# Borders and landing place of the last pieces of a streaming load, moved to multiples of 512 bytes

## The chip, the cores and the metric

One core of one Trainium2 chip. The time is the device time of one execution in microseconds (us). Differences here are far below 2%, so besides times I read landing events (when a transfer's semaphore is full) and packet records (bytes, start and duration of each DMA packet) of the traces, and compare two profiles of one kernel first.

## The reference

```python
x = np.random.randn(32, 512, 1024).astype(np.float32)      # 64 MB
out = np.sum(np.maximum(x, 0), axis=-1)                     # 32 x 512 sums
```

## The kernel before

The 16384 rows of 1024 numbers are spread over 128 partitions, 128 rows each. Loads stream into a buffer of three places of 16 rows; ScalarE applies the maximum, VectorE sums, and for the last rows both do maximum and sum in one instruction per row. What matters here is the end: rows come in transfers of 8, 4 and 2, and the last two rows are cut into four pieces.

```python
buf = nc.alloc_sbuf_tensor("buf", [P, NB, BIG, D], fp32)      # starts at byte 16512 of a partition
w = D - CUT                                                    # CUT = 912, HEAD = 256
seam = nc.alloc_sbuf_tensor("seam", [P, 2 + w + HEAD + 2], fp32)
...
first, second, third = [(0, CUT), (D + D // 2, 2 * D), (D + HEAD, D + D // 2)]
for k, (lo, hi) in enumerate((first, second, third)):
    sp.dma_start(out=flat[:, lo:hi], in_=rows[:, lo:hi]).then_inc(...)
sp.dma_start(out=seam[:, 2 : 2 + w + HEAD], in_=rows[:, CUT : D + HEAD]).then_inc(s_seam, 16)
...
on_act(flat[:, lo : CUT // 2], seam[:, 0:1]).then_inc(s_half, 1)      # halves of the first piece
on_dve(flat[:, CUT // 2 : hi], seam[:, 1:2]).then_inc(s_half, 1)
...                                                                    # second: ScalarE; third: VectorE
act.wait_ge(s_seam, 16 + 2)                                            # seam landed, both others summed
act.wait_ge(s_half, 2)
on_act(seam[:, 0:k], res[:, J - 2 : J - 1]).then_inc(s_last, 1)        # k = 2 + w
dve.wait_ge(s_seam, 16 + 2)
on_dve(seam[:, k : k + HEAD + 2], res[:, J - 1 : J]).then_inc(s_last, 1)
```

The seam holds the end of the last row but one and the start of the last row, with the partial sums of the other pieces in the columns beside them, so that one instruction for each row closes its sum. Then the last store goes out. In the build the big buffer starts 128 bytes past a multiple of 512 (16512 = 32 x 512 + 128), and so does the seam tensor (213120); the seam's data starts two columns later, at byte 136 of a block.

Of the kernel before, what the change touches and what calls it, by code (L numbers as in the profile page):

```python
# [3 lines left out]
P = 128  # L4
D = 1024
# [4 lines left out]
ACT_STEPS = [[16], [7, 9], [7, 9], [7, 9], [4, 5, 7], [3, 4, 5]]  # L10
DVE_STEPS = [[4, 5, 7], [7, 4, 5], [7, 4, 5], [7, 4, 5], [4, 5, 7], [3, 4, 5]]
TAIL = [8, 4, 2]
CUT = 912
HEAD = 256


def bass_relu_sum_kernel(
# [14 lines left out]
    fp32 = mybir.dt.float32  # L32
# [5 lines left out]
    J = B * S // P  # L38
# [11 lines left out]

    buf = nc.alloc_sbuf_tensor("buf", [P, NB, BIG, D], fp32)
    w = D - CUT
    seam = nc.alloc_sbuf_tensor("seam", [P, 2 + w + HEAD + 2], fp32)
    res = nc.alloc_sbuf_tensor("res", [P, J], fp32)
    turned = nc.alloc_sbuf_tensor("turned", [P, 32], fp32)

# [6 lines left out]
    s_half = nc.alloc_semaphore("s_half")  # L63
    s_seam = nc.alloc_semaphore("s_seam")
    s_last = nc.alloc_semaphore("s_last")
# [4 lines left out]
    sp, act, dve = nc.sync, nc.scalar, nc.vector  # L70
# [14 lines left out]
    for c in range(NBIG + 1):  # L85
        if c >= NB:
            sp.wait_ge(s_dve, done[c - NB])
        if c < NBIG:
            i = 0
            for g, j, n in CHUNKS[c]:  # L90
                sp.dma_start(  # L91
                    out=buf[:, c % NB, i : i + n, :], in_=xv[g][:, j : j + n, :]
# [14 lines left out]

    rows = xv[-1].rearrange("p j d -> p (j d)")[:, r * D : (r + 2) * D]
    flat = buf[:, tb, r : r + 2, :].rearrange("p j d -> p (j d)")
    first, second, third = [(0, CUT), (D + D // 2, 2 * D), (D + HEAD, D + D // 2)]  # L110
    for k, (lo, hi) in enumerate((first, second, third)):
        sp.dma_start(out=flat[:, lo:hi], in_=rows[:, lo:hi]).then_inc(  # L112
            s_in[NBIG + len(TAIL) + k], 16
        )
    sp.dma_start(out=seam[:, 2 : 2 + w + HEAD], in_=rows[:, CUT : D + HEAD]).then_inc(s_seam, 16)
    sp.wait_ge(s_turn, 1)
    sp.dma_start(
        out=of[0:P].rearrange("(k q) -> k q", q=32), in_=turned[0:P:32, 0:32]
# [7 lines left out]
    def on_act(t, acc):  # L126
        return act.activation(t, t, AF.Relu, accum_out=acc)  # L127

    def on_dve(t, acc):
        return dve.tensor_scalar(  # L130
            out=t, in0=t, scalar1=0.0, scalar2=None, op0=ALU.max, op1=ALU.add, accum_out=acc
        )
# [4 lines left out]
    k = 0  # L137
    for c in range(NTWO):
# [17 lines left out]
        for n in DVE_STEPS[c]:  # L156
            if ready[r + n - 1] > seen:
# [3 lines left out]
                out=res[:, c * BIG + r : c * BIG + r + n],  # L161
                in_=buf[:, c % NB, r : r + n, :],
# [24 lines left out]
    lo, hi = first  # L187
    act.wait_ge(s_in[-3], 16)
    dve.wait_ge(s_in[-3], 16)
    on_act(flat[:, lo : CUT // 2], seam[:, 0:1]).then_inc(s_half, 1)  # L190
    on_dve(flat[:, CUT // 2 : hi], seam[:, 1:2]).then_inc(s_half, 1)
    k = 2 + w
    lo, hi = second
    act.wait_ge(s_in[-2], 16)
    on_act(flat[:, lo:hi], seam[:, k + HEAD : k + HEAD + 1]).then_inc(s_seam, 1)
    lo, hi = third
    dve.wait_ge(s_in[-1], 16)
    on_dve(flat[:, lo:hi], seam[:, k + HEAD + 1 : k + HEAD + 2]).then_inc(s_seam, 1)
    act.wait_ge(s_seam, 16 + 2)
    act.wait_ge(s_half, 2)  # L200
    on_act(seam[:, 0:k], res[:, J - 2 : J - 1]).then_inc(s_last, 1)
    dve.wait_ge(s_seam, 16 + 2)
    on_dve(seam[:, k : k + HEAD + 2], res[:, J - 1 : J]).then_inc(s_last, 1)

# [33 lines left out]
```

## Time and profile before

The median is 160.83 us. In the trace:

| transfer (issue order) | bytes per partition | landed at, us | from the last packet's end to the landing, us |
|---|---|---|---|
| 4 rows | 16384 | 152.301 | 0.42 |
| 2 rows | 8192 | 154.814 | 0.48 |
| first piece | 3648 | 155.934 | 0.48 |
| second piece | 2048 | 156.626 | 0.53 |
| third piece | 1024 | 156.988 | 0.55 |
| seam | 1472 | 157.438 | 0.47 |
| last store | 64 | 159.349 | 0.38 |

A packet record ends when the engine has done with the packet; the landing is what the program waits for. The distance between the two is 0.42 to 0.55 us for the first five loads and 0.47 us for the seam. The chain of waits and the last instructions are shown in the prediction.

### The profile page before, as it was taken

What the parts mean: (1) busy time and instruction counts of PE and PEld (TensorE: products, weight loads), DVE (VectorE), ACT (ScalarE), POOL (GpSimd) and SP (SyncE); (2) the same over time, 40 slices, a digit from 0 to 9 for tenths busy, and PEclk for the clock granted to TensorE, in tenths of its full rate; (3) what the DMA queues carried; (4) which work ended last, traced back from release to release, by engine and by line L of the source; (5) the groups of instructions that cost most, each with busy time, mean ns of one, the idle gap of its engine ahead of it and who ended that gap; (6) DMA issues with size and microseconds to landing.
All of it is one profiled execution on the core that took longest, in us unless ns stands there. A gap on an engine that the chain in (4) does not pass through costs nothing.

```text
span 159.4 us, 150 instructions
## 1 busy us (share of the span) xinstructions
DVE 120.6 (76%) x59; ACT 101.5 (64%) x54; POOL 0.2 (0%) x4
## 2 busy tenths in 40 slices
DVE  0000000009999999999999999999999999898995
ACT  3000059980799708996099941999329980496975
POOL 0000000000000000000000000000000000000000
DMA  9997996996996997989979969969969979798994
GB/s 378 493 401 339 493 526 263 526 526 263 526 493 296 526 444 345 526 378 411 526 312 477 526 263 526 526 263 526 526 263 526 444 345 526 321 469 374 417 400 142
DMA packets 2457, 67.18 MB, mean 421 GB/s; under 512 B 536, under 2 KB 792, under 8 KB 1176
## 3 DMA queue, kind: packets, MB, share of 16 engines
q1 hardware_dynamic: 2456, 67.18, 98.1%
q14 instruction: 1, 0.01, 0.0%
HBM read 67.11 MB, written 0.07 MB: 421 GB/s over the span
## 4 chain that ended last, share of the span: by engine, by line
DVE 55%; DMA 34%; ACT 9%; SPq 2%; issue 0%
DVE res L160 54%; DMA buf<-in_x_dram 34%; ACT buf L145 9%; SPq L101 1%; SPq L112 1%; DVE buf L130 0%; DVE seam L130 0%; SPq L91 0%; DVE turned L169 0%
## 5 line engine op out<-in xcount | busy, mean ns | idle before, releaser
L160 DVE TENSOR_REDUCE res<-buf 128x4 f32<-128x4096 f32 (+3 forms) x18 | 99.4, 5596 | 35.5 <-ACT buf L145 35.5
L145 ACT ACTIVATE buf<-buf 128x7168 f32<-128x7168 f32 (+5 forms) x13 | 80.4, 6233 | 46.1 <-DMA buf<-in_x_dram 46.1
L127 ACT ACTIVATE buf<-buf 128x1024 f32<-128x1024 f32 (+2 forms) x19 | 19.0, 999 | 8.9 <-DMA buf<-in_x_dram 8.9
L130 DVE TENSOR_SCALAR_CACHE_REDUCE buf<-buf 128x1024 f32<-128x1024 f32 (+2 forms) x19 | 20.7, 1143 | 1.7 <-DMA buf<-in_x_dram 1.6
L127 ACT ACTIVATION_READ_ACCUMULATOR buf<-buf 128x1 f32 x19 | 3.6, 188 | 0.0
L145 ACT ACT_TABLE_LOAD x1 | 1.3, 1283 | 1.3 <-PEq L223 1.3
L130 DVE DVE_READ_ACCUMULATOR buf<-buf 128x1 f32 x19 | 1.6, 84 | 0.0
L130 DVE TENSOR_SCALAR_CACHE_REDUCE seam<-seam 128x258 f32<-128x258 f32 x1 | 0.4, 421 | 0.0
L127 ACT ACTIVATE seam<-seam 128x114 f32<-128x114 f32 x1 | 0.3, 300 | 0.1
L169 DVE STREAM_TRANSPOSE turned<-res 128x32 f32<-128x32 f32 x1 | 0.2, 211 | 0.0
L127 ACT ACTIVATION_READ_ACCUMULATOR seam<-seam 128x1 f32 x1 | 0.2, 186 | 0.0
L223 POOL MEMSET const-bfloat16-1.0<- 128x1 bf16 x1 | 0.1, 101 | 0.0
L223 POOL MEMSET const-uint8-127<- 128x1 uint8 x1 | 0.1, 101 | 0.0
L223 POOL MEMSET const-float32-0.0<- 128x1 f32 x1 | 0.1, 98 | 0.2 <-issue 0.2
L223 POOL MEMSET const-float32-1.0<- 128x1 f32 x1 | 0.1, 98 | 0.0
L130 DVE DVE_READ_ACCUMULATOR seam<-seam 128x1 f32 x1 | 0.1, 82 | 0.0
## 6 DMA issues: line engine op xcount, KB each, us to landing
buf<-in_x_dram SPq DMA_DIRECT2D x1, 7680.0 KB, 21.1
buf<-in_x_dram SPq DMA_DIRECT2D x1, 4096.0 KB, 25.3
buf<-in_x_dram SPq DMA_DIRECT2D x1, 2048.0 KB, 29.9
buf<-in_x_dram SPq DMA_DIRECT2D x1, 1024.0 KB, 31.9
buf<-in_x_dram SPq DMA_DIRECT2D x1, 512.0 KB, 3.3
buf<-in_x_dram SPq DMA_DIRECT2D x1, 456.0 KB, 32.5
buf<-in_x_dram SPq DMA_DIRECT2D x1, 256.0 KB, 32.7
seam<-in_x_dram SPq DMA_DIRECT2D x1, 184.0 KB, 32.6
```

The costliest lines, as they stand in the source:

```text
L101: sp.dma_start(out=buf[:, tb, r : r + n, :], in_=xv[-1][:, r : r + n, :]).then_inc(s_in[NBIG + i], 16)
L112: sp.dma_start(out=flat[:, lo:hi], in_=rows[:, lo:hi]).then_inc(s_in[NBIG + len(TAIL) + k], 16)
L127: return act.activation(t, t, AF.Relu, accum_out=acc)
L130: return dve.tensor_scalar(out=t, in0=t, scalar1=0.0, scalar2=None, op0=ALU.max, op1=ALU.add, accum_out=acc)
L145: act.activation(t, t, AF.Relu).then_inc(s_act, 1)
L160: dve.tensor_reduce(out=res[:, c * BIG + r : c * BIG + r + n], in_=buf[:, c % NB, r : r + n, :], axis=X, op=ALU.add,).then_inc(s_dve, 1)
L169: dve.transpose(out=turned[:, :], in_=res[:, 0:32]).then_inc(s_turn, 1)
L223: nc = _bacc.Bacc("TRN2", target_bir_lowering=False, num_devices=1)
```

## The change

The intent: let every piece of the last two rows begin and end at a multiple of 512 bytes in memory, and let the seam land on one, its partial sums just in front of it (96 columns are 384 bytes, and 128 + 384 = 512).

```diff
-CUT = 912
+CUT = 896
 HEAD = 256
+MID = 512
...
-    seam = nc.alloc_sbuf_tensor("seam", [P, 2 + w + HEAD + 2], fp32)
+    z = 96
+    seam = nc.alloc_sbuf_tensor("seam", [P, z + w + HEAD + 2], fp32)
...
-    first, second, third = [(0, CUT), (D + D // 2, 2 * D), (D + HEAD, D + D // 2)]
+    first, second, third = [(0, CUT), (D + MID, 2 * D), (D + HEAD, D + MID)]
...
-    sp.dma_start(out=seam[:, 2 : 2 + w + HEAD], in_=rows[:, CUT : D + HEAD]).then_inc(s_seam, 16)
+    sp.dma_start(out=seam[:, z : z + w + HEAD], in_=rows[:, CUT : D + HEAD]).then_inc(s_seam, 16)
...
-    on_act(flat[:, lo : CUT // 2], seam[:, 0:1]).then_inc(s_half, 1)
-    on_dve(flat[:, CUT // 2 : hi], seam[:, 1:2]).then_inc(s_half, 1)
-    k = 2 + w
+    on_act(flat[:, lo : CUT // 2], seam[:, z - 2 : z - 1]).then_inc(s_half, 1)
+    on_dve(flat[:, CUT // 2 : hi], seam[:, z - 1 : z]).then_inc(s_half, 1)
+    k = z + w
...
-    on_act(seam[:, 0:k], res[:, J - 2 : J - 1]).then_inc(s_last, 1)
+    on_act(seam[:, z - 2 : k], res[:, J - 2 : J - 1]).then_inc(s_last, 1)
```

## The prediction

> **What bounds the kernel now.** I read the page first (parts 1, 2 and 3), then the chain of waits, then the DMA issues, then the instructions of the last microseconds in order of time, and at last the trace's packet records, landing by landing.
>
> ```profile
> span 159.4 us, 150 instructions
> DVE 120.6 (76%) x59; ACT 101.5 (64%) x54; POOL 0.2 (0%) x4
> DMA packets 2457, 67.18 MB, mean 421 GB/s; under 512 B 536, under 2 KB 792, under 8 KB 1176
> q1 hardware_dynamic: 2456, 67.18, 98.1%
> ```
>
> The reader is to see that the 16 DMA engines are busy for 98.1% of the span and neither compute engine for more than 76%. The kernel is one long load. Only the end, after the last bytes have come, can be shortened by arranging things, and the end is all that the change touches. The packet counts say more than they seem to: 536 packets under 512 B are 276 four-byte semaphore writes, 128 of 64 B and 128 of 444 B (stores) and 4 of 128 B; adding 128 of 1024 B and 128 of 1472 B gives 792; adding 128 each of 2048, 3648 and 4096 B gives 1176. So the 3648-byte piece and the 1472-byte piece each go as one packet per partition. They aren't cut at 512-byte borders, and there is no short remainder packet for the change to remove.
>
> The chain of waits, cut to the last stretch:
>
> ```profile
> 5 pieces in order of time: start us, us, what
> 124.39 32.60 DMA buf<-in_x_dram
> 156.99 0.02 issue
> 157.01 0.44 DVE buf L130 x2
> 157.45 0.02 issue
> 157.47 0.43 DVE seam L130 x2
> ```
>
> It names the 256-column piece (the one of 1024 B per partition, third of four): it lands at 156.99, VectorE reduces it until 157.44, then the last two reductions start. The chain hides a near tie. In the landing events of the trace the 1472-byte "seam" piece, issued last, lands at 157.438 us, and VectorE's third piece ends at 157.442. The final reductions wait for both. Whoever speeds up one alone gains 4 ns and no more.
>
> The last instructions in order of time:
>
> ```profile
> 157.01 0.42 DVE L130 TENSOR_SCALAR_CACHE_REDUCE buf<-buf 128x256 f32<-128x256 f32 x1 [0.40 <-DMA buf<-in_x_dram]
> 157.08 0.34 SPq L123 DMA_DIRECT2D out_dram<-res  x1
> 157.19 0.19 ACT L127 ACTIVATION_READ_ACCUMULATOR buf<-buf 128x1 f32 x1
> 157.36 0.08 DVE L130 DVE_READ_ACCUMULATOR buf<-buf 128x1 f32 x1
> 157.47 0.30 ACT L127 ACTIVATE seam<-seam 128x114 f32<-128x114 f32 x1
> 157.47 0.42 DVE L130 TENSOR_SCALAR_CACHE_REDUCE seam<-seam 128x258 f32<-128x258 f32 x1
> 157.68 0.19 ACT L127 ACTIVATION_READ_ACCUMULATOR seam<-seam 128x1 f32 x1
> 157.82 0.08 DVE L130 DVE_READ_ACCUMULATOR seam<-seam 128x1 f32 x1
> 157.93 0.34 SPq L207 DMA_DIRECT2D out_dram<-res  x1
> ```
>
> ScalarE's final sum ends at 157.87, VectorE's at 157.90; the store is issued at 157.93 and lands at 159.35, 1.42 us later. After that nothing is left.
>
> **What the Trainium skill says, and whether the trace agrees.** "DMA: Bandwidth & Descriptors", section "Specifications", gives 512 B as the smallest transfer at line rate, with read-modify-write below it. That is a size, and all four pieces are above it before and after; only the stores (64 B and 444 B per partition) are below. Section "How a descriptor splits into AXI transactions" of the same page says that a descriptor is cut at 256-byte borders, that a beat is 32 B, and that one which starts off such a border also fetches the bytes back to it. This is the only stated mechanism by which the change can help. The packet records let it be tested below. Section "Anatomy of one DMA — SWDGE (gpsimd) path" puts most of a fixed 2 us into the receipt of the last write. Here the queue is another one, and from the last data packet's end to the last semaphore increment I find 0.42 us (packets of 16384 B), 0.48 (3648 B), 0.53 (2048 B), 0.55 (1024 B) and 0.47 (1472 B): the misaligned piece pays no longer receipt than its neighbours. "SBUF — State Buffer", section "Operand start alignment", says of odd start addresses only that they are legal, and that nothing was timed.
>
> **The change, part by part.** No instruction, wait or transfer is added or removed on any engine; the comparison of instruction orders shows the same 23, 18 and 13 rows on VectorE, ScalarE and the queue, with only sizes changed (456 to 448 twice, 114 to 130, 912 to 896, 368 to 384).
>
> 1. The first piece goes from 3648 to 3584 B per partition, the seam from 1472 to 1536: the same bytes in all. A long packet costs per byte (2418 - 309 ns) / (65536 - 8192 B) = 0.0368 ns on its engine. I divide the time between the ends of successive pieces by the 8 packets that each engine moves of each: 1.116 us / 8 = 139.5 ns for 3648 B, 0.647 / 8 = 80.9 for 2048, 0.344 / 8 = 43.0 for 1024, 0.526 / 8 = 65.8 for 1472. Taking off the bytes (134.2, 75.3, 37.7, 54.1) leaves 5.3, 5.6, 5.3 and 11.7 ns. So three pieces have a fixed part of 5.4 ns, the 3648-byte one among them, although its end is off any 512-byte border; only the seam pays more, about 6.3 ns a packet. The skill's beats agree with that size: the seam is written from byte 136 of a 512-byte block (the tensor starts at 128 of one in the build, and two columns are kept free), which taken from the border below makes 51 beats instead of 46, and 5 beats of 32 B at 0.0368 ns/B are 5.9 ns. They don't explain all: the pieces in the big buffer also land at byte 128 of a block, and pay nothing that can be told from their fixed part.
>
> 2. So the first piece ends 8 x 64 B x 0.0368 = 19 ns sooner, and the second and third with it: the third lands at 156.97. The seam itself has 19 ns more bytes and 8 x 6.3 = 50 ns less of excess: it lands at 157.438 - 0.050 = 157.39.
>
> 3. VectorE's third piece starts 19 ns earlier and, with 0.44 us as before, ends at 157.42. The seam is now 30 ns ahead of it, so the gain on the path is VectorE's 19 ns, not the 50 of the transfer. The last reductions start at 157.45.
>
> 4. VectorE's half of the first piece loses 8 columns and ScalarE's too, some 7 ns each; both had ended well before the third piece landed (156.6). Nothing on the path.
>
> 5. The final sums: VectorE keeps 258 columns (0.42 us). ScalarE goes from 114 to 130. From 114 columns in 300 ns and 512 in 630 it costs 0.83 ns a column, so 13 ns more. It had ended some 40 ns ahead of VectorE and still ends first, by 25. Nothing on the path.
>
> 6. A side effect that the diff doesn't show: the seam tensor grows from 1488 to 1928 B, so the result tensor behind it moves by 448 B. The last store reads 64 B per partition; before from byte 32 of a 256-byte block, after from byte 224, so over a border. By the skill's counting this makes 9 beats instead of 3; 6 x 32 B x 0.0368 = 7 ns a packet, and with 8 packets per engine at most 57 ns, if nothing in the writing side hides it. The packets now take 10.4 ns each; I put in half of the worst case, 25 ns.
>
> Sum on the path: -19 + 25 = about nothing; without the side effect -0.02 us, with it in full +0.04. From 160.83 I predict 160.82 us.
>
> **The rivals.** First, that the whole 50 ns of the seam reach the end: this needs VectorE's third piece not to be in the way, and the tie of 157.438 against 157.442 speaks against it; it would give 160.78. Second, that misaligned writes are dearer than the packet durations show, through a delayed receipt or by slowing the neighbours on the same engines (the rate falls from about 427 GB/s, 65536 B in 2418 ns on 16 engines, to near 360 in the seam's stretch). The equal receipts speak against the first half. The falling rate is explained by fixed parts of ever shorter packets. If it were so, up to 0.3 us could go: 160.5. Third, that the last store gets slower as in step 6, or the middle store of 444 B, whose start moves from byte 100 to byte 36 of a block. The middle one has its last landing at 159.05, before 159.35, so it has room; the last one has none: up to 160.87. Fourth, that ScalarE becomes the last with its longer sum; the margin of 40 ns against 13 speaks against it, and if wrong it costs less than 20 ns.
>
> **Range and chances.** All rivals lie between 160.5 and 160.9. The three runs before spread from 160.83 to 161.05, and the profiled one had 160.74, so the range is that of the noise: 160.5 to 161.1. A change of 2% would be 3.2 us, more than everything that follows the last data (159.39 - 156.97 = 2.4 us); I see no way to it in either direction except another state of the chip. Faster by over 2%: 0.01; within: 0.98; slower: 0.01.
>
> **What would show it.** In the changed profile the packet counts should again be 536, 792 and 1176. Steps 1 and 2: the seam's packets of 1536 B should take about as long as or less than those of 1472 B did (67.5 ns on average as recorded), and its landing should come about 0.40 to 0.42 us after the third piece's, where it was 0.45. Step 3: the chain should go through VectorE's third piece still, with the final sums starting 0.48 us after its landing as now. Step 5: ScalarE's sum over 130 columns near 313 ns. Step 6: from the last store's issue to its landing 1.42 to 1.48 us. What would make it wrong: a last landing moved by more than 0.1 us either way, a seam that still lands last (then alignment bought nothing), or a store longer by over 0.1 us.

## The result, and the profile after

The median after is 160.82 us (160.72 to 161.31, 6 runs), before 160.83 (160.75 to 161.05, 6 runs). The ratio is 1.0002, 95% interval 0.9988 to 1.0015: the same. (A ratio is the mean time of one kernel's fast runs over that of the other's of the same rounds, so not quite the ratio of the medians.)

From the page of the changed kernel:

```profile
span 159.4 us, 150 instructions
...
DMA packets 2457, 67.18 MB, mean 422 GB/s; under 512 B 536, under 2 KB 792, under 8 KB 1176
...
q1 hardware_dynamic: 2456, 67.18, 98.1%
```

The packet counts are the same three numbers as before, so no packet has gone. Its chain of waits, the last stretch (start, duration, what):

```profile
124.37 32.60 DMA buf<-in_x_dram
156.97 0.02 issue
156.99 0.44 DVE buf L133 x2
157.43 0.02 issue
157.46 0.43 DVE seam L133 x2
```

The chain still goes through the third piece and VectorE, everything 0.01 to 0.02 us sooner. The last instructions in order of time (line numbers are 3 higher in this kernel):

```profile
156.99 0.42 DVE L133 TENSOR_SCALAR_CACHE_REDUCE buf<-buf 128x256 f32<-128x256 f32 x1 [0.36 <-DMA buf<-in_x_dram]
...
157.46 0.31 ACT L130 ACTIVATE seam<-seam 128x130 f32<-128x130 f32 x1
157.46 0.42 DVE L133 TENSOR_SCALAR_CACHE_REDUCE seam<-seam 128x258 f32<-128x258 f32 x1
...
157.91 0.34 SPq L210 DMA_DIRECT2D out_dram<-res  x1
```

ScalarE's longer sum takes 0.31 us instead of 0.30 and stays ahead of VectorE. The seam landed at 157.422 and VectorE's third piece ended at 157.424: the tie is still a tie, where I had expected the seam 30 ns ahead. The seam came 0.452 us after the third piece; I had predicted 0.40 to 0.42. The store took 1.413 us from issue to landing, 1.417 before. This first pair of traces looks like the predicted 19 ns. The experiments ask whether it is, and why the seam did not come out of the tie.

### The profile page after: what moved, and what is told of

Same layout as the page of the kernel before. It is cut to its first block, busy times and chain, and to the rows that moved or that the text cites. A ratio compares the mean times of both kernels' runs of the same rounds, so it can differ in the third digit from the quotient of the medians.

```text
span 159.4 us, 150 instructions
## 1 busy us (share of the span) xinstructions
DVE 120.6 (76%) x59; ACT 101.5 (64%) x54; POOL 0.2 (0%) x4
## 4 chain that ended last, share of the span: by engine, by line
DVE 55%; DMA 34%; ACT 9%; SPq 2%; issue 0%
DVE res L163 54%; DMA buf<-in_x_dram 34%; ACT buf L148 9%; SPq L104 1%; SPq L115 1%; DVE buf L133 0%; DVE seam L133 0%; SPq L94 0%; DVE turned L172 0%
```

## The experiments

### Noise: the kernel before, once more

No edit.

> The kernel before, unchanged, to learn how far two profiles of one kernel differ. No theory is at stake. I expect the third piece's landing, the seam's landing and the final sums' start within 0.03 us of the first profile (156.99, 157.44, 157.47), the recorded mean of the 1472-byte packets within 1.5 ns of 67.5, and of the 64-byte store packets within 1.5 ns of 10.4. If they scatter by more, the 18 ns by which the changed kernel's end came sooner cannot be told from noise.

Measured: 160.81 us. The chain of waits:

```profile
157.05 0.02 issue
157.08 0.44 DVE buf L130 x2
157.52 0.02 issue
157.54 0.43 DVE seam L130 x2
```

Everything lies 0.065 us later than in the first profile of the same program, more than the 0.03 I had allowed, and over three times the predicted gain. The shift is there from the first chunk's landing on (21.651 against 21.587). So the 18 ns of the first pair prove nothing by themselves. What repeats are distances: from the landing of chunk 6 (the last of 16 rows) to that of the third piece 19.288 and 19.279 us, from the third's to the seam's 0.450 and 0.448, and the mean recorded packet of 1472 B 67.5 and 68.4 ns. From here on I compare such distances.

### The border alone

```diff
 (kernel before)
-CUT = 912
+CUT = 896
```

> One half of the change: the border between the first piece and the seam goes from column 912 to 896, the landing stays at byte 136 of a 512-byte block. Theory A (position in the stream: the first piece is 64 B shorter, so the third lands 19 ns sooner and VectorE's reduction of it gates the end): the third piece lands near 156.97 and the final sums start near 157.45, as in the changed kernel. Theory B (alignment of the landing is what pays): as before, 156.99 and 157.47, and the seam lands at 157.44. The seam's 1536-byte packets: 69 ns by A, as in the changed kernel, over 71 by B.

Measured: 160.84 us. The third piece came 19.305 us after chunk 6, not sooner but about 20 ns later than in the kernel before, and the final sums started at 157.57; neither theory foresaw this. The seam came 0.469 us after the third, which is 0.449 plus the 19 ns of its longer packets, and those took 72.4 ns, theory B's number (over 71, against 69 by A), in one profile.

### The landing alone

```diff
 (changed kernel)
-CUT = 896
+CUT = 912
```

> The other half: the border stays at column 912, the seam lands at a multiple of 512 bytes with the partial sums beside it. Theory A: third piece 156.99, final sums 157.47, 1472-byte packets still 67 to 68 ns. Theory B: the packets fall to some 62 ns (the bytes at 0.0368 ns plus 7.7 ns) and the seam lands at 157.39 instead of 157.44; the final sums may still start at 157.47 because VectorE is in the way.

Measured: 161.13 us, with the seam's packets at 62.0 ns, exactly their bytes plus the constant: theory B's number. But this execution had a disturbance: packets of 16384 and 3648 B took up to 0.84 and 0.50 us where 0.61 and 0.14 are normal, and the first piece came 0.4 us late. Such a pause also lets any backlog drain, so this run alone decides nothing on the packets. And the seam landed 0.455 us after the third piece, no sooner than in the kernel before (0.450 and 0.448), where theory B had 0.40: cheaper packets as recorded, but no earlier landing.

### The seam third instead of last

```diff
 (kernel before)
     for k, (lo, hi) in enumerate((first, second, third)):
+        if k == 2:
+            sp.dma_start(out=seam[:, 2 : 2 + w + HEAD], in_=rows[:, CUT : D + HEAD]).then_inc(s_seam, 16)
         sp.dma_start(out=flat[:, lo:hi], ...)
-    sp.dma_start(out=seam[:, 2 : 2 + w + HEAD], ...)
```

> The kernel before with the seam issued third and the 256-column piece last; nothing else changes. It asks whom the extra 5 to 6 ns of a seam packet belong to. If to its addresses, the 1472-byte packets stay at 67 to 68 ns and the 1024-byte ones at 46. If to being last in the queue, the 1472-byte ones fall to 63 to 64 and the 1024-byte ones rise to 50 to 52. In both cases the last piece lands near 157.44, VectorE then reduces it until about 157.89 and the final sums start there, so the kernel ends some 0.4 us later, near 161.2.

Measured: 161.28 us and final sums at 158.00, close to the expectation. The 1472-byte packets fell to 64.6 ns, the 1024-byte ones, now last, rose only to 47.5. So about half of the seam's excess went with the position and half stayed with the packets; neither clean answer.

### Which of the two opens the final sums

```diff
 (changed kernel)
-MID = 512
+MID = 576
```

> The changed kernel with the border between second and third piece at column 576 instead of 512: the third has 320 columns, the second 448; the third and the seam land when they did. If VectorE's reduction of the third piece opens the final sums, its 64 more columns (1.04 ns each) move the sums' start from 0.48 us after the third's landing to 0.55 us. If the seam's landing opens them (rival), they start 0.03 us after it, as now, 0.48 after the third's landing.

Measured: 160.84 us, and the chain of waits:

```profile
157.01 0.02 issue
157.04 0.51 DVE buf L133 x2
157.54 0.02 issue
157.57 0.43 DVE seam L133 x2
```

With 64 more columns VectorE's part of the chain is 0.51 us instead of 0.44, and the sums start 0.55 us after the third's landing (157.015) although the seam was there at 157.464, as before 0.45 us after the third. So VectorE's reduction of the third piece opens the final sums when it ends after the seam's landing. A faster seam could gain nothing beyond the tie: step 3's argument holds.

### The disputed cost by itself

The loads of chunks 3 to 6 of the kernel before are cut into 32 runs of 368 columns (1472 B, the seam's size) per partition; each of the 16 engines then moves 8 x 32 = 256 such packets per chunk, back to back. The sums are wrong; only the loads matter.

```diff
 (kernel before)
+RUNS = {3: (96, 0), 4: (2, 16), 5: (2, 0), 6: (96, 16)}    # chunk: (column to land at, column to read from)
...
+    to, src = buf[:, c % NB, i : i + n, :], xv[g][:, j : j + n, :]
+    if c in RUNS:
+        at, fro = RUNS[c]
+        to, src = (t.rearrange("p j (h d) -> p (j h) d", h=2)[:, :, o : o + 368]
+                   for t, o in ((to, at), (src, fro)))
-    sp.dma_start(out=buf[:, c % NB, i : i + n, :], in_=xv[g][:, j : j + n, :]).then_inc(s_in[c], 16)
+    sp.dma_start(out=to, in_=src).then_inc(s_in[c], 16)
```

The second kernel has `{3: (2, 16), 4: (0, 0), 5: (1, 1), 6: (96, 0)}`, the third `{3: (98, 0), 4: (112, 0), 5: (114, 0), 6: (32, 0)}`. As the buffer starts at byte 128 of a block, column c is byte 128 + 4c.

> The disputed cost by itself, wrong results on purpose: the loads of chunks 3 to 6 are cut into runs of 368 columns (1472 B), 32 of them per partition, each from half a row into half a row; so each of 16 engines moves 256 packets of the seam's size per chunk, back to back. Chunk 3 starts at multiples of 512 B on both sides; chunk 4 as the seam before (64 B past in memory, landing at byte 136); chunk 5 off on the landing side alone; chunk 6 off in memory alone. Theory A (alignment is free): all four chunks take the same, near 8 x 32 x 62 to 68 ns = 16 to 17.4 us, within 1%. Theory B (a packet off the multiples pays 5 to 6 ns): chunks 4 and 5 take 1.3 to 1.5 us longer than chunk 3, and chunk 6 some 0.6 us if the two extra beats in memory count.

> The same with other places and in another order: chunk 3 as the seam before, chunk 4 from a multiple of 512 B to byte 128 of a block (where everything in the big buffer lands), chunk 5 off by 4 B against that on both sides, chunk 6 on multiples of 512 B on both sides. Theory A: all the same within 1% and the same as in the other order. Theory B: chunk 6 fastest, chunk 3 and 5 slowest by 5 to 6 ns a packet (1.3 to 1.5 us), chunk 4 in between or equal to chunk 6.

The stretches of 12 us inside chunks 3, 4, 5 and 6 of the first of these kernels (columns: stretch and its length, busy us of VectorE, ScalarE and GpSimd, granted clock, DMA busy share, GB/s):

```profile
62.00:74.00 12.00, 11.96 (x4) 12.00 (x2) 0.00 (x0) 1.00 1.05 400
77.00:89.00 12.00, 12.00 (x4) 12.00 (x2) 0.00 (x0) 1.00 1.06 358
94.00:106.00 12.00, 12.00 (x4) 12.00 (x3) 0.00 (x0) 1.00 1.06 358
110.50:122.50 12.00, 12.00 (x3) 11.44 (x7) 0.00 (x0) 1.00 1.05 400
```

and of the second:

```profile
62.00:74.00 12.00, 11.96 (x4) 12.00 (x2) 0.00 (x0) 1.00 1.06 358
79.00:91.00 12.00, 12.00 (x3) 12.00 (x2) 0.00 (x0) 1.00 1.06 357
96.00:108.00 12.00, 12.00 (x3) 12.00 (x3) 0.00 (x0) 1.00 1.06 358
112.00:124.00 12.00, 12.00 (x5) 11.83 (x7) 0.00 (x0) 1.00 1.05 400
```

There are two rates and nothing in between. An offset of 64 bytes in memory costs nothing (last line of the first). Landing at byte 128, 132 or 136 costs a tenth of the rate, and byte 128, where everything in the big buffer lands, is as dear as the two others (second and third line of the second). Here the packet records follow: 62.0 ns on average in the fast stretches, 69.8 to 70.0 in the slow ones. So theory A, that alignment is free, is dead, and so is theory B's charge for an offset in memory, at least for this one.

> Again runs of 1472 B, all from multiples of 512 B in memory, wrong results on purpose; only the landing byte within a 512-byte block differs: chunk 3 at byte 8, chunk 4 at byte 64 (it ends exactly on a block's end), chunk 5 at byte 72 (it ends 8 B past it), chunk 6 at byte 256. Theory S (the start must be on a multiple): chunks 3, 4 and 5 take 16.85 us. Theory N (the number of blocks touched counts, one more costs 7 ns a packet): chunks 3 and 4 take 15.0 us like the aligned ones (3 blocks of 512 B, or 6 of 256), chunk 5 16.85. Chunk 6 tells the block: 15.0 us if 256 B (6 blocks of 256), 16.85 if 512 B (4 blocks instead of 3).

```profile
62.00:74.00 12.00, 11.96 (x4) 12.00 (x2) 0.00 (x0) 1.00 1.05 400
77.00:89.00 12.00, 12.00 (x4) 12.00 (x2) 0.00 (x0) 1.00 1.05 400
93.00:105.00 12.00, 12.00 (x4) 11.73 (x3) 0.00 (x0) 1.00 1.06 357
109.00:121.00 12.00, 12.00 (x3) 11.51 (x7) 0.00 (x0) 1.00 1.05 400
```

Bytes 8 and 64 are as good as a multiple of 512, byte 72 is not, byte 256 is. Taken together, with the time between a chunk's landing and the one before it:

| kernel, chunk | landing byte in a 512-byte block | blocks of 256 B that 1472 B touch | us for the chunk |
|---|---|---|---|
| 1st, 3 | 0 | 6 | 15.07 |
| 1st, 6 (read 64 B off) | 0 | 6 | 14.93 |
| 2nd, 6 | 0 | 6 | 14.96 |
| 3rd, 3 | 8 | 6 | 15.06 |
| 3rd, 4 | 64 | 6 | 15.02 |
| 3rd, 6 | 256 | 6 | 15.06 |
| 2nd, 4 | 128 | 7 | 16.87 |
| 2nd, 5 (read 4 B off) | 132 | 7 | 16.84 |
| 1st, 5 | 136 | 7 | 16.84 |
| 1st, 4; 2nd, 3 (read 64 B off) | 136 | 7 | 16.83; 16.83 |
| 3rd, 5 | 72 | 7 | 17.11 |

Theory N fits every row: what counts is how many 256-byte blocks of the landing a packet touches, not where it starts. (The 17.11 has some extra delay at its ends; inside the stretch its rate is that of the other slow ones.) The five other slow values average 16.84 us, the fast ones 15.02: 1.82 us / 256 = 7.1 ns for one more block. This is for 1472 B only. An estimate from these numbers: a slow packet takes 16.84 us / 256 = 65.8 ns, and 7 blocks of 256 B at the long packets' 0.0368 ns/B are 65.9; so a block touched in part seems to take the time of a full one. Six blocks would be 56.5 ns, but the fast packets take 15.02 / 256 = 58.7, so something else holds them there. Other sizes were not tried back to back. Whether a reading side that touches one more block costs as much is not tried: the two read offsets keep the number at 6.

### The big buffer moved by 8 and by 384 bytes

```diff
 (kernel before; 8 bytes)
-    buf = nc.alloc_sbuf_tensor("buf", [P, NB, BIG, D], fp32)
+    whole = nc.alloc_sbuf_tensor("buf", [P, 2 + NB * BIG * D], fp32)
+    buf = whole[:, 2:].rearrange("p (b j d) -> p b j d", b=NB, j=BIG)
```

```diff
 (kernel before; 384 bytes)
+    nc.alloc_sbuf_tensor("pad", [P, 96], fp32)
     buf = nc.alloc_sbuf_tensor("buf", [P, NB, BIG, D], fp32)
```

> The kernel before with its big buffer 8 bytes further: all loads but the seam now land at byte 136 of a 512-byte block, as the seam did. If an off landing costs once per packet, 5 to 6 ns on 10 + 3 packets per partition, 8 partitions per engine, make 0.5 to 0.6 us: 161.4. If it cost once per 256-byte step, the whole stream would be many us longer. If it costs nothing: 160.8, ratio within 0.2% of 1.

> The kernel before with its big buffer 384 bytes further, so that all loads but the seam land on multiples of 512 B instead of at byte 128 of a block: what the change does for one piece of 1472 B, done for all the rest of the 64 MB. If byte 128 costs 4 beats a packet (4.7 ns), some 0.4 to 0.5 us come back: 160.35. If it costs nothing: 160.8, ratio within 0.2% of 1, and the 1024- and 2048-byte packets take 46 and 84 ns as they did.

Measured for 8 bytes: 160.89 us against 160.94, ratio 0.9995 (0.9978 to 1.0012). By theory N this is no change at all, since a transfer of a multiple of 256 B touches one block too many at byte 136 as at byte 128.

Measured for 384 bytes: 160.66 us (160.58 to 160.78, 4 runs) against 160.94 (160.78 to 161.20, 7 runs), ratio 0.9982, interval 0.9968 to 0.9997: small, and clear of 1. It is less than the 0.4 to 0.5 us that I expected if byte 128 costs anything. (The pad moves the seam too: in the build it starts at 213504, a multiple of 512, and its data at byte 8 of a block, where 1472 B touch 6 blocks instead of 7. So every load but the first piece touches one block fewer here, not only those into the buffer.) Its chain of waits:

```profile
124.48 32.32 DMA buf<-in_x_dram
156.81 0.02 issue
156.83 0.44 DVE buf L131 x2
157.27 0.02 issue
157.29 0.43 DVE seam L131 x2
```

The third piece lands 0.18 us sooner than in the first profile of before. The distances between landings show where it comes from: 16384 B 4.833 us instead of 4.895 (mean of before's two profiles), 8192 B 2.455 instead of 2.504, second piece 0.629 instead of 0.697, third 0.301 instead of 0.358: each time 0.05 to 0.07 us, where 8 packets of 7.1 ns are 0.057. (The first piece, 3648 B, touches 15 blocks in either place; it came 1.17 us after its neighbour instead of 1.12, so 0.05 later. The seam, with one block fewer, came 0.460 us after the third, not sooner than before.) The recorded packet durations of the other pieces hardly moved (medians of 46 and 84 ns for 1024 and 2048 B, as in before); the landings did. Only the seam's packets fell, from 67.5 to 62.0 ns. And the distance from last packet to landing, which grew from 0.42 to 0.55 us in before, is now flat: 0.31, 0.32, 0.37, 0.36, 0.31, 0.30.

### Everything on multiples of 512

```diff
 (changed kernel)
+    nc.alloc_sbuf_tensor("pad", [P, 96], fp32)
     buf = nc.alloc_sbuf_tensor("buf", [P, NB, BIG, D], fp32)
...
-    z = 96
+    z = 128
```

> The changed kernel with the big buffer also moved by 384 bytes, so that every load of the kernel lands on a multiple of 512 B (and the seam is moved so that it stays on one). Theory: what pays is how many loads land so, not this one piece; in the last six pieces 8 packets x 7 ns = 0.056 us each, 0.34 us in all, less what the long packets before have hidden. So 0.2 to 0.35 us under the kernel before, ratio 0.998, like the one with the buffer alone moved; clear of 1 but far from 2%. The landing of the last piece comes near 157.25 us, and the final sums wait for it or for VectorE within 0.03 us. Rival (nothing pays, the other one was luck of the run): ratio 1.000.

Measured: 160.73 us (160.64 to 160.94, 5 runs) against 160.79 (160.78 to 161.11, 9 runs), ratio 0.9993, interval 0.9979 to 1.0006: unclear whether it is faster at all. I had expected 0.2 to 0.35 us, clear of 1; the times don't bear this out. In the trace the tail is as short as with the buffer alone: from chunk 6's landing to the seam's 19.508 us (buffer alone 19.515; before 19.738 and 19.727; changed kernel 19.717 and 19.690). In this profile some of that was lost again elsewhere: chunk 6 landed at 137.839 instead of 137.70, and the last store took 1.518 us instead of 1.42. So a shorter tail by 0.22 us is seen in both traces. How much it is depends on where one begins to count: in both, chunk 6 itself landed 0.08 to 0.09 us later after chunk 5 than in before, and from chunk 5's landing to the seam's the gain is 0.12 and 0.14 us, from chunk 1's 0.23 in both. That a shorter tail makes the kernel faster is measured for one of the two.

### The changed kernel, once more

No edit.

> The changed kernel once more. Its absolute times I expect only within 0.07 us of the first profile, as with the kernel before. What should repeat, if the change does anything at all: the 1536-byte packets at 69 ns (72 with the border alone moved), the time from the third's landing to the seam's at 0.45 us (0.47 with the border alone), the final sums 0.48 us after the third's landing, and the store 1.41 us. The 64-byte store packets at 8.5 ns should repeat if they hang on the moved result tensor, and go back to 10.4 if they were chance.

Measured: 161.25 us. The 1536-byte packets took 69.3 ns again, the third piece came 19.258 us after chunk 6 (19.265 in the first profile), the seam 0.432 us after the third (0.452), the final sums 0.48 us after it. VectorE ended its third piece some 19 ns after the seam's landing this time. The last store took 1.742 us, 0.33 more than in the first profile, which is most of the lengthening of this run. The 64-byte packets took 8.3 ns, short again.

## Why the prediction was right or wrong

**The time**: 160.82 predicted and measured, the same within 0.15%. That the number was hit to the digit is luck: it is a sum of -19 and +25 ns, neither of which the runs confirm, and both lie under the 0.065 us by which two profiles of one kernel differ.

**The bound and the tie** were right: the longer third piece moved the end by its own 0.07 us with the seam already there.

**Step 1 is the step that failed.** It charged the seam's whole 6.3 ns above the fixed part of 5.4 ns to the seam's own landing, and said that the pieces in the big buffer "pay nothing that can be told from their fixed part". They do pay, but not there: with the buffer on the grid the ends of their packets still give 139.6, 80.9 and 43.0 ns, so the same fixed part, while all but the first piece land 0.05 to 0.07 us sooner after the load before them. The yardstick couldn't see the fault. And the seam's excess was in part its neighbours': its 1536-byte packets took 72.4 ns with everything off the grid, 67.7 to 69.3 with the seam alone on it (three profiles), 65.0 with the buffer on it too. So some 3 to 5 ns hang on the seam's landing and 3 to 4 on the others' (one profile each for the first and the last figure). By step 1's own division nothing is left over 5.4 ns in the two kernels with the buffer moved (0.476 us / 8 less 54.1 for 1472 B). The skill's section on how a descriptor splits gave the right grid, and I used it only for the seam, in beats. The trace had shown a sign: the distance from last packet to landing grew over the pieces. I read it as "the misaligned piece pays no longer receipt than its neighbours", but the neighbours were misaligned too; this second yardstick did have the fault. With nearly all landings on the grid the distances are flat near 0.3 us. That writes fall behind reads and the packet records see only part of it would explain this; it is argued, not shown.

**Step 2** expected 50 ns from the seam's alignment. Theory N gives 8 x 7.1 = 57 ns (7 blocks to 6). Against the border alone, which has the same 1536 bytes, the seam's distance to the third fell from 0.469 to 0.452 and 0.432, so by 17 to 37 ns, where two profiles of one kernel differ by 20; the predicted 0.40 to 0.42 was not reached. At 1472 B the seam on the grid came 0.455 and 0.460 us after the third, off it 0.448 to 0.460: no gain in landing. So the cheaper packets are seen, and an earlier landing of the seam by its own alignment is not shown. Why it doesn't follow stays open.

**Step 2's 19 ns and step 3's gain on the path** are not confirmed. The third piece came on average 22 ns sooner in the changed kernel's two traces (19.262 against 19.284 us after chunk 6), but with the border alone 21 ns later. This is as small as the scatter.

**Step 5** was right: 311 ns for 130 columns, predicted 313. **Step 4** was right as far as can be seen: both halves were done before the third landed.

**Step 6** stays open. The store took 1.413 and 1.742, 1.412, and 1.518 us in the four profiles whose result tensor straddles a 256-byte border at its end (the changed kernel twice, the longer third piece, everything on 512), and 1.412 to 1.422 in the ten others. So there is no steady charge of 25 ns, and the 64-byte packets were recorded shorter in all four (8.3 to 8.5 ns against 10.4 to 10.5), the opposite of the estimate. Whether the two slow ones are chance, or a rare penalty of that place, four profiles do not tell; the unchanged kernel has runs of 161.1 and 161.2 us too, but of the changed kernel's seven runs two lie above that (161.25 and 161.31).

**The second rival** was dismissed for the wrong reason. Misaligned writes are dearer than the packet durations show, and some 0.2 us of the tail could be had, by moving all loads (0.28 us in the medians of one such kernel, 0.06 and unclear in the other). This change moved one load of the tail, and that one stood in a tie. One sum of this rival is wrong too: 65536 B in 2418 ns on 16 engines are 434 GB/s, not 427; the argument doesn't hang on it.

## What to carry to other kernels

Count how many 256-byte blocks each packet touches where it lands; a buffer that starts 128 bytes off makes each packet whose length is a multiple of 256 touch one too many. It cost a tenth of the rate at 1472-byte packets, so look to the start address of the big buffer before you polish one piece, and don't expect to see it with long packets. When you measure whether a fault costs anything, check that the yardstick can see it (here the landings did, and the packets' ends did not) and that what you compare with doesn't have it.

## What the Trainium skill lacked or had wrong

- "DMA: Bandwidth & Descriptors", section "Specifications": 512 B as the smallest size at line rate says nothing of the landing place. Packets of 1472 B, well above that size, ran at 400 or at 357 to 358 GB/s depending on it alone.
- The same page, section "How a descriptor splits into AXI transactions": it tells of fetching, and the same 256-byte grid holds on the landing side. There the number of blocks sets the cost and not the beats: landing at byte 64 makes 48 beats instead of 46 by its counting, and cost nothing (15.02 against 15.02 us on average); one more block cost 7.1 ns a packet. The section gives no time for a block.
- "SBUF — State Buffer", section "Operand start alignment", says that its runs timed nothing. Here is a time: a start 8 or 64 bytes past a 256-byte border cost a packet of 1472 B nothing, one 72, 128, 132 or 136 bytes past it 7.1 ns, because its end then reaches into one more block.
- No page that I read gives a figure for how far landings can move while the packet durations recorded by the profiler stay: 0.05 to 0.07 us a piece here (1024 and 2048 B: medians of 46 and 84 ns in both kernels).
